# Up product: ten tiles in seven products instead of eight

## The chip, the cores and the metric

The kernel runs on one core of a Trainium2 chip. A core has five engines with a queue each: TensorE (PE in the profile; its weight loads are shown apart as PEld), VectorE (DVE), ScalarE (ACT), GpSimd (POOL) and SyncE (SP, which here only issues transfers). They wait for each other by semaphores. Matmul results land in PSUM, which has eight banks of 128 x 512 float32; everything else is in SBUF.

The metric is the device time of one execution in microseconds (us), as the median of several runs.

## The reference

One layer on x (1, 512, 1024) in float32: a mixing part (retention and a gated unit), then a gated MLP with a short convolution. The change touches the MLP:

```python
def _conv_gated_mlp(h, w_up, conv_w, conv_b, w_down):
    hid = h @ w_up                       # (512, 1024) @ (1024, 5632)
    hid = conv_general_dilated(hid, conv_w, ...) + conv_b   # 3 positions, each column by itself
    a, b = jnp.split(hid, 2, axis=-1)
    return (jax.nn.gelu(a) * b) @ w_down # (512, 2816) @ (2816, 1024)

h2 = _rmsnorm(x, g_pre_ffn)
x = x + _rmsnorm(_conv_gated_mlp(h2, w_up, conv_w, conv_b, w_down), g_post_ffn)
```

## The kernel before

**Number format.** Each operand is split into a high part (`hi`, rounded by an ACT copy, L85) and a low part (`lo`, the rest, by a DVE subtraction, L92). One product is three matmuls: high by high, high by low, low by high (`mm3`, L230).

**The up product.** Its 5632 columns are 22 tiles of 2 x 128: tile i holds the columns a and b that `gelu(a) * b` needs, as weight blocks 2i and 2i+1 of 128 x 1024 (eight pieces of 128 along the contraction). The result is held transposed, 128 columns by 512 positions.

A *whole* tile is two `up_block` calls (L954). Each takes one block (two slots, `hi` and `lo`) and one PSUM bank, and issues 8 x 3 matmuls of 512 columns: 48 matmuls of 512 for a tile.

A tile as a *pair* (class `Pair`, L675) is computed in the manner of Strassen and Winograd: seeing the two blocks, the two halves of the contraction and the two halves of the positions as a 2 x 2 product, it takes seven products of half the size in place of eight. Each is 4 x 3 matmuls of 256 columns: 84 matmuls of 256 for a tile. It needs weight forms B11, B21, T1 to T4 and B22 (`w_form`, L159), one slot each. T1 and T3 are sums made by DVE (L170, L171), T2 and T4 by POOL (L172, L174). Each of the seven forms is then split. On the other side stand forms of h2 (`h2forms`), made once.

A pair's seven products come in three parts, in three banks:
- `part1`: B11 into bank `b[0]` (ACT copies it out), B21 into `b[1]` (DVE adds it), T1 into `b[2]`, and T2 added into `b[0]`, which ACT copies out again (`copy(c1[:, T0], o)`, L711)
- `part2`: T3 added into `b[0]` (L717), ACT copies it out, DVE subtracts (L719). It also fetches the weights of the next part.
- `part3`: T4 added into `b[0]`, copied out by ACT; B22 added into `b[2]`, DVE subtracts (L731)

**The order around it.** `COUPLES` (L42) names eight couples of tiles, 4 to 19. In a couple the first tile is a pair and the second is whole: `part1`, first block, `part2`, second block with `part3` in its middle. Tiles 0 to 3, 20 and 21 are whole. After a tile `tile_done` (L1043) runs the convolution (ACT L997, DVE L1000 and L1004, for a and for b), the gelu (ACT L1011) and the product (DVE L1013). After tiles 7, 11, 13, 17 and 19 it also calls `down_forms` (L1024), which makes the operand forms of one pair of tiles for the down product: on DVE five steps of 256 and three of 512, on ACT four copies.

**Weights.** `units` (L99 to L123) lists what is prepared, in order: `("blk", i)` a block, `(form, i)` a form. `w_get` (L220) hands out the next unit and lets units be issued ahead up to nine slots (tag `w4`, nine buffers, L130). Loads go to `raw` tiles of 512 KB (four buffers, L127), issued by SP. `_up` (L1291) lays out the blocks of pair tiles in halves on the host.

**Who sets the order.** The program is handed to a framework that finds the dependencies, places tiles in free buffers of their tag and sets the order of each engine's instructions. The order written in the code is a priority there, not a fixed sequence. Temporaries (`tmp`) have six buffers, PSUM eight.

Of the kernel before, what the change touches and what calls it, by code (L numbers as in the profile page):

```python
# [38 lines left out]
ENDS = (0, 2, 3, 1)  # L39
UP0 = DOWN0 - 2 * NF  # L40
EARLY = 4
COUPLES = [(i, i + 1) for i in range(4, 20, 2)]  # L42

PRE, LNG, LNB = 0, 8, 16
CW, CB = 24, 24 + 3 * 2 * NF
# [5 lines left out]
def tile_block(ctx: ExitStack, tc, xT, x, wall, par, cs, wsp, bsp, gpost, gpre, gffn, out):  # L51
# [11 lines left out]
    def blk(dt=F32, n="blk", shape=(P, S)):  # L63
        return sb.tile(list(shape), dt, tag="blk", bufs=NBLK, name=nm(n))
# [4 lines left out]
    def tmp(n="tmp", shape=(P, S)):  # L69
        return sb.tile(list(shape), F32, tag="tmp", bufs=6, name=nm(n))  # L70
# [7 lines left out]
    def ps(shape=(P, S)):  # L78
        return pp.tile(list(shape), F32, tag="ps", name=nm("ps"))
# [18 lines left out]
    FORMS = ("B11", "B21", "T1", "T2", "T3", "T4", "B22")  # L98
    units = []  # L99
    i = 0  # L100
    while i < NW:
        pair = [(f, i) for f in FORMS]
        if U0 <= i < GATE0:
            units += pair
            i += 2
        elif GATE0 <= i < GATE1:
            units += pair[:4] + [("blk", i + 2)] + pair[4:] + [("blk", i + 3)]
            i += 4
        elif i == UP0 + 2 * COUPLES[0][0]:
            for a, b in COUPLES:  # L110
                pair = [(f, UP0 + 2 * a) for f in FORMS]
                units += pair[:4] + [("blk", UP0 + 2 * b)] + pair[4:] + [("blk", UP0 + 2 * b + 1)]
            i = UP0 + 2 * COUPLES[-1][1] + 2
        elif i == DOWN0:
            for _ in range(2):
                pairs = [[("q", i + j), ("t", i + j)] for j in range(DP)]
                whole = [[("blk", i + DP)], [("blk", i + DP + 1)]]
                for u in pairs[:4] + whole[:1] + pairs[4:6] + whole[1:] + pairs[6:] if i == DOWN0 else pairs + whole:
                    units += u
                i += DP + WHOLE // 2  # L120
        else:
            units.append(("blk", i))
            i += 1  # L123
# [90 lines left out]
    def w_next():  # L214
        u = units[w_pos[1]]
        w_ready[w_pos[1]] = w_unit(u)
        w_pos[1] += 1
        return w_size(u)

    def w_get(look=LOOK, most=99):  # L220

        i = w_pos[0]
        w_pos[0] += 1
        room = 2 * look + (2 if w_size(units[i]) == 2 else 0)
        n = sum(w_size(u) for u in units[i : w_pos[1]])
        while w_pos[1] < len(units) and (w_pos[1] <= i or n + w_size(units[w_pos[1]]) <= min(most, max(room, 9 if look == LOOK else 0))):
            n += w_next()
        return w_ready.pop(i)

    def mm3(o, ah, al, bh, bl, start, stop):  # L230
        nc.tensor.matmul(o, ah, bh, start=start, stop=False)  # L231
        nc.tensor.matmul(o, ah, bl, start=False, stop=False)  # L232
        nc.tensor.matmul(o, al, bh, start=False, stop=stop)  # L233
# [48 lines left out]
    for k in range(KD):  # L282
# [18 lines left out]
        for m in range(8):  # L301
            c = slice(m * P, (m + 1) * P)
# [78 lines left out]
    for m in range(8):  # L381
        t = blk(n="qkraw")
# [266 lines left out]
    for n, acc in enumerate(t_group()):  # L649
        if n == 0:  # L650
            g_turn(0)
        if n < 2:
            for k in (n + 2, n + 6):
                t = tmp("xT")
# [92 lines left out]
    uT, late = [], None  # L747
    for j in range(KD // 2):
        p = Pair(AF.Gelu_apprx_tanh, lambda: blk(n="u"), scale=rbc)
# [7 lines left out]
        late = p  # L757
# [46 lines left out]
    for j in range(KD // 2):  # L804
        for o, t in gated_pair(ogh, ogl, late if j == 0 else None):
            b = blk(n="r")
# [117 lines left out]
    def h2(k, t):  # L924
        return tuple(h[k // 2][:, k % 2, t] for h in (h2h, h2l))

    h2forms = {n: [None] * 4 for n in ("S1", "S2", "S3", "S4")}
# [8 lines left out]
    def h2_sums(i):  # L936

        a0, b0, a1, b1 = h2r[0][i], h2r[0][i + 2], h2r[1][i], h2r[1][i + 2]
        v.tensor_sub(b1, a1, b1)
        v.tensor_sub(a1, a0, a1)  # L940
        v.tensor_sub(a0, b1, a0)
        v.tensor_add(b0, b0, a0)
        for n, t in zip(("S1", "S2", "S3", "S4"), (b1, a0, a1, b0)):
            h2_parts(n, i, t)
# [9 lines left out]
    def up_block(between=None):  # L954
        (wh, wl), o = w_get(), ps()
        for k in range(KD):
            if between and k == KD // 2:
                between()
            c = slice(k * P, (k + 1) * P)
            mm3(o, wh[:, c], wl[:, c], *h2(k, slice(0, S)), k == 0, k == KD - 1)  # L960
        return o
# [33 lines left out]
    def conv(o, m):  # L995
        c = tmp("cv")
        nc.scalar.activation(  # L997
            out=c, in_=o, func=AF.Identity, scale=col(CW + 3 * m + 1), bias=col(CB + m)
        )
        v.scalar_tensor_tensor(  # L1000
            out=c[:, 1:S], in0=o[:, 0 : S - 1], scalar=col(CW + 3 * m), in1=c[:, 1:S],
            op0=ALU.mult, op1=ALU.add,
        )
        v.scalar_tensor_tensor(  # L1004
            out=c[:, 0 : S - 1], in0=o[:, 1:S], scalar=col(CW + 3 * m + 2), in1=c[:, 0 : S - 1],
            op0=ALU.mult, op1=ALU.add,
        )
        return c

    def gated(ca, cb):  # L1010
        nc.scalar.activation(out=ca, in_=ca, func=AF.Gelu_apprx_tanh)  # L1011
        gp.append(blk(n="gp"))
        v.tensor_mul(gp[-1], ca, cb)  # L1013
# [10 lines left out]
    def down_forms(j):  # L1024

        a, b = gp[2 * j], gp[2 * j + 1]
        first = blk(F32R, "fa")
        split(first[:, T0], first[:, T1], a[:, T0])
        s_ = blk(n="fs")
        v.tensor_sub(s_[:, T0], a[:, T1], b[:, T1])  # L1030
        v.tensor_sub(s_[:, T1], s_[:, T0], a[:, T0])
        v.tensor_sub(a[:, T0], a[:, T0], a[:, T1])
        v.tensor_add(a[:, T1], b[:, T0], s_[:, T1])
        bh, bl = two_parts(b, j >= WIDE)
        sh, sl = two_parts(s_, j >= WIDE)
        th, tl = two_parts(a, j >= WIDE)
        dforms.append({
            "A11": (first[:, T0], first[:, T1]), "A12": (bh[:, T0], bl[:, T0]), "A22": (bh[:, T1], bl[:, T1]),
            "S1": (sh[:, T0], sl[:, T0]), "S2": (sh[:, T1], sl[:, T1]),
            "S3": (th[:, T0], tl[:, T0]), "S4": (th[:, T1], tl[:, T1]),  # L1040
        })

    def tile_done(i, o):  # L1043
        gated(*(conv(t, 2 * i + s_) for s_, t in enumerate(o)))
        if i < COUPLES[-1][1]:
            if i in (7, 11, 13, 17):
                down_forms(len(dforms))
        elif len(dforms) < EAGER:
            down_forms(len(dforms))

    couples = dict(COUPLES)
    i = 0
    while i < NF:
        if i in couples:
            p = Pair(None, lambda: tmp("c"), h2, h2forms)
            p.part1()
            o = [up_block()]
            p.part2()
            o.append(up_block(p.part3))
            tile_done(i, p.t)  # L1060
            tile_done(i + 1, o)
            i += 2
        else:
            o = []
            for e in (2 * i, 2 * i + 1):
                o.append(early_o[e] if e < EARLY else up_block())
            if i < 2:
                h2_sums(i)
                w_next()
            tile_done(i, o)  # L1070
            i += 1
# [154 lines left out]
    for t in ENDS:  # L1226
# [10 lines left out]
        for i, (b, e) in enumerate((((M2, e1), (M3, xx)), ((M4, uu), (M8, yy)))[t // 2]):  # L1237
            f, h = slice((t % 2) * 256, (t % 2 + 1) * 256), slice(i * 256, (i + 1) * 256)
# [14 lines left out]
        if t in ADDED:  # L1253
            o = blk(n="o")
# [35 lines left out]

def _up(a):  # L1291

    for i, _ in COUPLES:
        b, c = a[2 * i].reshape(P, 2, S), a[2 * i + 1].reshape(P, 2, S)
        a[2 * i : 2 * i + 2] = np.stack([
            np.concatenate([b[:, 0], c[:, 0]], -1), np.concatenate([c[:, 1], b[:, 1]], -1),
        ])
    return a
# [85 lines left out]
```

## Time and profile before

| | us |
|---|---|
| median of 3 runs | 818.92 |
| lowest, highest | 818.67, 819.13 |
| the profiled execution | 818.99 |
| its span | 817.2 |
| PE busy | 810.2 |
| DVE busy | 657.0 |
| ACT busy | 430.0 |

The span runs from the first to the last instruction that the profile shows; the execution's time has some more around it. Start times in a view are in us from the start of the span. The up product lies between about 471 and 703 us, tiles 4 to 19 between 517 and 681. Matmuls are pipelined: a matmul of 256 columns is shown with 0.28 us, but the next starts about 0.11 later, so PE's pace is read from starts, not from durations. Some matmul records are missing from the trace.

In a row of a view, `wf<-raw` names the tile written and the tiles read: `wf` is the high or low part of a form, `wh` and `wl` those of a block, `c` a pair's result, `cv` a convolution's, `ps` a PSUM bank. `[1.71 <-PE ps L691]` says that the engine had been idle for 1.71 us until that instruction of PE released it.

### The profile page before, as it was taken

How to read it: one execution, taken by the hardware profiler on the slowest of the kernel's cores; microseconds unless marked ns; L12 is line 12 of the kernel's file. 1: busy time of each engine (PE TensorE's matmuls, PEld its weight loads, DVE VectorE, ACT ScalarE, POOL GpSimd, SP SyncE). 2: the span in 40 equal slices, each digit the busy share in tenths (PEclk: the TensorE clock that was granted, in tenths of full speed). 3: DMA queues.
4: the chain of work that ended last, by engine and by line, in shares of the span. 5: the costliest groups of instructions: out<-in, count | busy, mean ns of one | idle time of the engine just before them, and what ended most of it. 6: DMA issues, size and time to landing. Idle time of an engine off the chain costs nothing.

```text
span 817.2 us, 13212 instructions
## 1 busy us (share of the span) xinstructions
PE 810.2 (99%) x5154; PEld 730.9 (89%) x5154; DVE 657.0 (80%) x1076; ACT 430.0 (53%) x733; POOL 102.5 (13%) x108
## 2 busy tenths in 40 slices
PE   9999999999999999999999999999999999999997
PEld 7888888888899999999988898899999998999996
DVE  7579897877898877767766579778989989898976
ACT  6636445536665544444435466455656665645532
POOL 0100000012222011132211210210201200000001
PEclk9999999999999999999999999999999999999999
DMA  8733221222234332323359212333333341234354
GB/s 284 262 117 103 77 79 65 68 75 79 91 101 133 104 93 88 103 86 103 102 175 360 87 49 73 104 103 103 104 104 103 103 140 67 78 103 129 104 181 104
DMA packets 29391, 93.76 MB, mean 115 GB/s; under 512 B 3408, under 2 KB 4304, under 8 KB 29328
## 3 DMA queue, kind: packets, MB, share of 16 engines
q1 hardware_dynamic: 26928, 86.59, 32.1%
q0 software_dynamic: 1968, 6.03, 2.4%
q8 instruction: 40, 0.66, 0.4%
q10 hardware_dynamic: 432, 0.30, 0.1%
q14 instruction: 23, 0.19, 0.1%
HBM read 88.19 MB, written 4.72 MB: 114 GB/s over the span
## 4 chain that ended last, share of the span: by engine, by line
PE 98%; DMA 0%; DVE 0%; issue 0%; ACT 0%; DVEq 0%
PE ps L691 23%; PE ps L232 13%; PE ps L231 13%; PE ps L233 13%; PE ps L1088 11%; PE ps L495 5%; PE ps L496 5%; PE ps L497 5%; PE ps L1119 2%; PE ps L846 2%; PE ps L845 2%; PE ps L847 2%; PE ps L770 1%; PE ps L295 1%; PE ps L912 0%; PE ps L620 0%
## 5 line engine op out<-in xcount | busy, mean ns | idle before, releaser
L92 DVE TENSOR_TENSOR wl<-raw,wh 128x1024 fp32r<-128x1024 f32 (+1 forms) x93 | 108.9, 1180 | 48.2 <-PE ps L691 24.2
L85 ACT ACTIVATE wf<-raw 128x512 fp32r<-128x512 f32 x140 | 84.9, 626 | 98.7 <-PE ps L232 40.2
L92 DVE TENSOR_TENSOR wf<-raw,wf 128x512 fp32r<-128x512 f32 x140 | 110.0, 802 | 26.4 <-ACT wf L85 25.6
L691 PE MATMUL ps<-sh,wf 128*128 128x256 f32 x640 | 118.8, 277 | 0.0
L85 ACT ACTIVATE wh<-raw 128x1024 fp32r<-128x1024 f32 (+2 forms) x95 | 93.0, 989 | 34.5 <-DMA raw<-wall 16.5
L691 PEld LDWEIGHTS ps<-sh,wf 128*128 128x128 f32 x640 | 100.7, 188 | 0.9 <-ACT wf L85 0.2
L231 PE MATMUL ps<-h2h,wh 128*128 128x512 f32 (+1 forms) x256 | 93.2, 364 | 0.0
L232 PE MATMUL ps<-h2l,wh 128*128 128x512 f32 (+1 forms) x256 | 93.1, 364 | 0.0
L233 PE MATMUL ps<-h2h,wl 128*128 128x512 f32 (+1 forms) x256 | 92.8, 362 | 0.0
L691 PE MATMUL ps<-sl,wf 128*128 128x256 f32 x320 | 88.5, 277 | 0.0
L495 PE MATMUL ps<-wh,xh 128*128 128x512 f32 x192 | 75.1, 391 | 0.0
L496 PE MATMUL ps<-wl,xh 128*128 128x512 f32 x192 | 74.9, 390 | 0.0
L497 PE MATMUL ps<-wh,xl 128*128 128x512 f32 x192 | 74.8, 390 | 0.0
L172 POOL TENSOR_TENSOR raw<-raw,raw 128x512 f32<-128x512 f32 x20 | 33.9, 1693 | 239.5 <-DVE raw L170 185.9
L691 PEld LDWEIGHTS ps<-sl,wf 128*128 128x128 f32 x320 | 60.1, 188 | 0.8 <-issue 0.2
L233 PEld LDWEIGHTS ps<-h2h,wl 128*128 128x128 f32 x256 | 48.3, 189 | 7.7
L231 PEld LDWEIGHTS ps<-h2h,wh 128*128 128x128 f32 x256 | 48.2, 188 | 6.9
L232 PEld LDWEIGHTS ps<-h2l,wh 128*128 128x128 f32 x256 | 48.1, 188 | 6.5
L691 PE MATMUL ps<-xh,wf 128*128 128x256 f32 x288 | 53.4, 278 | 0.0
L1088 PE MATMUL ps<-dl,fh 128*128 128x256 f32 x168 | 46.5, 277 | 0.0
L1088 PE MATMUL ps<-dh,fl 128*128 128x256 f32 x168 | 46.5, 277 | 0.0
L1088 PE MATMUL ps<-dh,fh 128*128 128x256 f32 x168 | 46.5, 277 | 0.0
(326 smaller groups left out, 2057.9 us busy)
## 6 DMA issues: line engine op xcount, KB each, us to landing
raw<-wall SPq DMA_DIRECT2D x145, 512.0 KB, 3.5
x<-x SPq DMA_DIRECT2D x20, 256.0 KB, 5.5
xT<-xT SPq DMA_DIRECT2D x8, 256.0 KB, 5.5
x<-x POOLq DMA_DIRECT2D x8, 256.0 KB, 2.6
xT<-xT POOLq DMA_DIRECT2D x4, 256.0 KB, 3.9
cs<-cs SPq DMA_DIRECT2D x2, 256.0 KB, 4.2
gpm<-gpost POOLq DMA_DIRECT2D x2, 256.0 KB, 3.9
gpr<-gpre POOLq DMA_DIRECT2D x2, 256.0 KB, 5.0
```

Of the source, the lines that this page charges most:

```text
L85: nc.scalar.activation(out=o, in_=i, func=AF.Copy)
L92: return nc.vector.tensor_sub(lo, src, as32(hi))
L172: nc.gpsimd.tensor_tensor(out=w_raw["T2"], in0=w_raw["T1"], in1=w_raw["B22"], op=ALU.add)
L231: nc.tensor.matmul(o, ah, bh, start=start, stop=False)
L232: nc.tensor.matmul(o, ah, bl, start=False, stop=False)
L233: nc.tensor.matmul(o, al, bh, start=False, stop=stop)
L495: nc.tensor.matmul(acc[t], xh[k][:, c], wh[:, f], start=k == 0, stop=False)
L496: nc.tensor.matmul(acc[t], xh[k][:, c], wl[:, f], start=False, stop=False)
L497: nc.tensor.matmul(acc[t], xl[k][:, c], wh[:, f], start=False, stop=k == KD - 1)
L691: nc.tensor.matmul(o, w_[:, c], a_, start=first and k == n == 0, stop=k == 3 and n == 2, skip_group_check=True,)
L845: nc.tensor.matmul(o, ah, bh, start=k == 0, stop=False)
L1088: nc.tensor.matmul(o, a_[:, c], w_[:, f], start=j == t == i == 0, stop=j == DP - 1 and i == 2 and n not in (M2, M3, M4), skip_group_check= ...
```

## The change

- `COUPLES` becomes `GROUPS`: four groups of three tiles (4 to 6, 7 to 9, 10 to 12, 13 to 15) and two couples (16, 17) and (18, 19). In a group of three the first two tiles are pairs and the third is whole. So ten tiles are pairs: 4, 5, 7, 8, 10, 11, 13, 14, 16, 18.
- The order in a group of three: first pair's `part1`, `part2`; second pair's `part1`; first pair's `part3` and `tile_done`; second pair's `part2`; first block of the whole tile; second block with the second pair's `part3` in its middle; `tile_done` for both. In the first pair `part2` follows `part1` with nothing between them.
- `units` lists 7 + 7 forms and then the two blocks for a group of three. For a couple it is as before.
- `down_forms` comes after tiles 9, 12, 15 and 17 (`SUMS_AT`) and 19, instead of 7, 11, 13, 17 and 19.
- `_up` lays out the blocks of all ten pair tiles.

```diff
-COUPLES = [(i, i + 1) for i in range(4, 20, 2)]
+GROUPS = [(i, i + 1, i + 2) for i in range(4, 16, 3)] + [(16, 17), (18, 19)]
+SUMS_AT = (9, 12, 15, 17)
...
-        elif i == UP0 + 2 * COUPLES[0][0]:
-            for a, b in COUPLES:
-                pair = [(f, UP0 + 2 * a) for f in FORMS]
-                units += pair[:4] + [("blk", UP0 + 2 * b)] + pair[4:] + [("blk", UP0 + 2 * b + 1)]
-            i = UP0 + 2 * COUPLES[-1][1] + 2
+        elif i == UP0 + 2 * GROUPS[0][0]:
+            for *a, b in GROUPS:
+                for t in a:
+                    units += [(f, UP0 + 2 * t) for f in FORMS]
+                units.insert(len(units) if a[1:] else len(units) - 3, ("blk", UP0 + 2 * b))
+                units.append(("blk", UP0 + 2 * b + 1))
+            i = UP0 + 2 * GROUPS[-1][-1] + 2
...
-        if i < COUPLES[-1][1]:
-            if i in (7, 11, 13, 17):
+        if i < GROUPS[-1][-1]:
+            if i in SUMS_AT:
                 down_forms(len(dforms))
...
-    couples = dict(COUPLES)
+    groups = {g[0]: g for g in GROUPS}
     i = 0
     while i < NF:
-        if i in couples:
+        if i in groups:
             p = Pair(None, lambda: tmp("c"), h2, h2forms)
             p.part1()
-            o = [up_block()]
-            p.part2()
+            if len(groups[i]) > 2:
+                p.part2()
+                late, p = p, Pair(None, lambda: tmp("c"), h2, h2forms)
+                p.part1()
+                late.part3()
+                tile_done(i, late.t)
+                i += 1
+                p.part2()
+                o = [up_block()]
+            else:
+                o = [up_block()]
+                p.part2()
             o.append(up_block(p.part3))
             tile_done(i, p.t)
             tile_done(i + 1, o)
...
-    for i, _ in COUPLES:
+    for i in (t for g in GROUPS for t in g[:-1]):
```

## The prediction

> **What bounds the kernel now.** I read the page first, then TensorE's waits.
>
> ```profile
> span 817.2 us, 13212 instructions
> PE 810.2 (99%) x5154; PEld 730.9 (89%) x5154; DVE 657.0 (80%) x1076; ACT 430.0 (53%) x733; POOL 102.5 (13%) x108
> ...
> PE 98%; DMA 0%; DVE 0%; issue 0%; ACT 0%; DVEq 0%
> ```
>
> ```profile
> PE ps L280 <- DVE raw L275: 1.0, 1, 1.0
> ```
>
> PE is busy for 99% of the span, the chain that ended last is PE for 98%, and the second fence is the whole list of PE's waits: one, 1.0 us, at the start. So PE has no wait anywhere in the up product. Time can be won there only by giving PE less to do, and lost by making it wait.
>
> Next the windows view over the up product. Columns: window, its length, then busy time (instructions) of PE, PEld, DVE, ACT, POOL, then clock and DMA.
>
> ```profile
> 517.00:537.50 20.50, 20.50 (x133) 18.57 (x132) 13.88 (x20) 10.49 (x19) 2.93 (x2) 1.00 0.28 96
> 537.50:558.00 20.50, 20.50 (x133) 18.57 (x132) 15.70 (x25) 11.20 (x20) 2.94 (x2) 1.00 0.32 103
> 558.00:578.50 20.50, 20.50 (x133) 18.57 (x132) 19.85 (x32) 12.70 (x23) 2.94 (x2) 1.00 0.28 87
> 619.50:640.00 20.50, 20.50 (x133) 18.57 (x132) 20.05 (x32) 12.47 (x24) 2.94 (x2) 1.00 0.32 96
> 681.00:702.80 21.80, 21.80 (x98) 18.04 (x97) 19.36 (x33) 11.36 (x17) 0.00 (x0) 1.00 0.17 54
> ```
>
> The first four rows are couples: one tile in seven products (a pair) and one whole tile, 20.50 us each, PE never idle. In a couple without `down_forms` DVE is busy for 15.70 us, in one with them for 19.85 to 20.05. The last row is tiles 20 and 21, both whole: 10.9 us each.
>
> **What the change saves on PE.** The chain in order of time gives the pieces of a pair (start, length, matmuls):
>
> ```profile
> 537.69 5.45 PE ps L691 x48
> 548.60 1.37 PE ps L691 x12
> 552.71 2.73 PE ps L691 x24
> ```
>
> ```profile
> 221.94 38.04 PE ps L691 x335
> ```
>
> A pair is 48 + 12 + 24 = 84 matmuls, 5.45 + 1.37 + 2.73 = 9.55 us. The last fence is the U stage, four pairs in a row: 38.04 / 335 = 0.1136 us a matmul, so pairs that follow each other cost no more. In a couple the whole tile then takes 20.50 - 9.55 = 10.95 us. Tiles 4 to 15 are six couples now, 6 x 20.50 = 123.0. After it they are four groups of 2 x 9.55 + 10.95 = 30.05, together 120.2. **Saved on PE: 2.8 us** (2.7 with the 10.9 of tiles 20 and 21). Tiles 16 to 19 and the down product keep their work and their order.
>
> **What the other engines get.** The groups of instructions by line, for 480 to 690 us (count, busy, mean ns):
>
> ```profile
> L92 DVE TENSOR_TENSOR wf<-raw,wf 128x512 fp32r<-128x512 f32 x56 | 42.4, 771 | 6.6 <-ACT wf L85 5.8
> L92 DVE TENSOR_TENSOR wl<-raw,wh 128x1024 fp32r<-128x1024 f32 x24 | 31.9, 1327 | 12.9 <-PE ps L691 7.6 <-issue 5.1 <-ACT wh L85 0.3
> L85 ACT ACTIVATE wf<-raw 128x512 fp32r<-128x512 f32 x56 | 34.2, 626 | 25.3 <-PE ps L232 11.8 <-POOL raw L172 6.2 <-DVE raw L171 3.8
> L85 ACT ACTIVATE wh<-raw 128x1024 fp32r<-128x1024 f32 x23 | 24.2, 1053 | 0.1
> L85 ACT ACTIVATE c<-ps 128x256 f32<-128x256 f32 x32 | 12.1, 379 | 26.5 <-PE ps L691 26.5
> L171 DVE TENSOR_TENSOR raw<-raw,raw 128x512 f32<-128x512 f32 x8 | 6.3, 782 | 0.2
> L170 DVE TENSOR_TENSOR raw<-raw 128x512 f32<-128x512 f32 x8 | 5.5, 690 | 0.0
> L719 DVE TENSOR_TENSOR c<-ps,c 128x256 f32<-128x256 f32 x8 | 3.4, 420 | 0.1
> ```
>
> A tile that turns from whole to pair adds on DVE seven `wf` subtractions, two sums of weights and three 256-wide steps, and drops two `wl`: 7 x 0.771 + 0.782 + 0.690 + 3 x 0.42 - 2 x 1.327 = 5.5 us. On ACT: 7 x 0.626 + 4 x 0.379 - 2 x 1.053 = 3.8 us. POOL gets two more additions per pair. SP issues the same two transfers of 512 KB per tile.
>
> With 15.70 for a couple, whole = (15.70 - 5.5) / 2 = 5.1 and pair = 10.6. A group is 26.3 us of DVE, and with `down_forms` (19.85 - 15.70 = 4.15) 30.5, against 30.05 of PE. The new `SUMS_AT` puts `down_forms` into the second, third and fourth group and couple (16, 17). DVE falls behind by about 0.4 us a group, 1.2 in all; couple (16, 17), 19.85 of 20.50, gives back 0.65. ACT has at most 12.7 + 8 of 30.
>
> What hides this is the lead of the weights:
>
> ```profile
> 574.67 2.00 DVE L92 TENSOR_TENSOR wl<-raw,wh 128x1024 fp32r<-128x1024 f32 x1 [0.46 <-PE ps L691]
> ```
>
> ```profile
> 583.97 0.39 PE L231 MATMUL ps<-h2h,wh 128*128 128x512 f32 x1
> ```
>
> This `wl` is ready at 576.67 and first used at 583.97, 7.3 us ahead. After it the shortest way is that of a second pair's first form: with nine slots held, its slot is free when the group before ends, and its matmuls come 6.8 us into the group. A copy, a subtraction and a sum (0.63 + 0.77 + 0.78) leave over 4 us for a lag of 1 to 2. The U stage says the same:
>
> ```profile
> 225.70:235.00 9.30, 9.30 (x84) 9.30 (x84) 9.20 (x15) 6.67 (x12) 1.80 (x2) 1.00 0.31 104
> ```
>
> In these 9.30 us DVE is busy for 9.20, and PE still has no idle time: a nearly full DVE doesn't by itself hold PE up.
>
> **The new wait.** In a couple a whole block stands between `part1` and `part2`. In a group of three the first pair's `part2` follows at once, and its product adds into the bank, `b[0]`, that `part1` has just filled and ACT must copy out (`copy(c1[:, T0], o)`). PE can't write until the copy is done. No row shows such a wait, so it is bounded: nothing below (a copy hidden by other matmuls), above by the copy's own rows.
>
> ```profile
> 542.86 0.28 PE L691 MATMUL ps<-sh,wf 128*128 128x256 f32 x1
> 542.97 0.40 PE L231 MATMUL ps<-h2h,wh 128*128 128x512 f32 x1
> ```
>
> ```profile
> 543.17 0.38 ACT L85 ACTIVATE c<-ps 128x256 f32<-128x256 f32 x1 [1.71 <-PE ps L691]
> ...
> 563.67 0.38 ACT L85 ACTIVATE c<-ps 128x256 f32<-128x256 f32 x1 [1.41 <-PE ps L691]
> ```
>
> The last product of `part1` issues at 542.86, the next matmul at 542.97, the copy ends at 543.55: 0.58 us. For the signal back I add 0.07, about twice the 0.03 from the last matmul's end (542.86 + 0.28) to the copy's start: 0.65. Four groups: 2.6 us, nearly all of the gain. Behind the waiting matmul stand the second pair's products, and the whole chain.
>
> Whether it is paid turns on PE's order. The framework sets each engine's order by what it reckons ready, as DVE shows:
>
> ```profile
> 537.15 0.75 DVE L1000 SCALAR_TENSOR_TENSOR cv<-c,part,cv 128x511 f32<-128x511 f32 x1
> 537.81 0.74 DVE L1000 SCALAR_TENSOR_TENSOR cv<-ps,part,cv 128x511 f32<-128x511 f32 x1
> 538.57 0.69 DVE L92 TENSOR_TENSOR wf<-raw,wf 128x512 fp32r<-128x512 f32 x1
> 539.17 0.74 DVE L1004 SCALAR_TENSOR_TENSOR cv<-c,part,cv 128x511 f32<-128x511 f32 x1
> ```
>
> The code has L1004 right behind L1000 for one tile; here the next tile's L1000 and a weight split go between, because L1004 wasn't ready. If PE is ordered so too, some five matmuls of the second pair's first product (0.11 us each, another bank, weights ready) move ahead of the waiting one and fill the gap. I take this, with 0.15 us left over per group, since the planned length of the copy need not be the real one: 4 x 0.15 = 0.6 (ends 0 and 2.6).
>
> [...]
>
> **Sum.** -2.8 + 0.6 = -2.2 us: span 815.0. The profiled execution took 818.99, 1.8 beyond its span, and stands 0.07 above the median: 816.8, against the median **816.7 us**. With 0 to 0.35 left per group, 816.1 to 817.5.
>
> **The rivals.**
> 1. *The wait is paid in full.* PE keeps the written order. For: no case of moved matmuls in the trace. Against: DVE's order above. -2.8 + 2.6: 818.7 (818.3 to 818.9), no change.
> 2. *The wait, and a split ahead of the copy*, the case on the slower side. In the U stage:
>
> ```profile
> 228.48 0.28 PE L691 MATMUL ps<-xh,wf 128*128 128x256 f32 x1
> ```
>
> ```profile
> 228.74 0.63 ACT L85 ACTIVATE wf<-raw 128x512 fp32r<-128x512 f32 x1 [0.74 <-PE ps L691]
> 229.28 0.37 ACT L85 ACTIVATE u<-ps 128x256 f32<-128x256 f32 x1
> ```
>
> `part1` ended at 228.48, but ACT did a split first, as the same matmul freed its slot, and the copy ended at 229.65: 1.2 us. In four groups 4.8 - 2.8 = +2.0: 820.9. With written order it is slower by over 0.2% from 1.1 us a wait. Against it: in the couples (543.17, 563.67) ACT stood idle and copied at once.
> 3. *DVE becomes the bound.* From the second group on it has 30.5 for 30.05, and in the first group the second pair's forms are wanted 6.8 us after the start instead of 20.5. If POOL's additions hold DVE longer than now, the lag outgrows 4 us. The 2.00 of the `wl` at 574.67 stands beside
>
> ```profile
> 574.29 1.30 POOL L174 TENSOR_TENSOR raw<-raw,raw 128x512 f32<-128x512 f32 x1 [1.47 <-DVE wf L92]
> ```
>
> and is 0.7 over the mean of its form. With 1.1 us more per pair, three groups reach 32.7: 8 late, less 4 of lead, less 2.8: +1.2, 820; 1 or 2 lost give 818 to 819. [...]
>
> **Chances.** Forecast 0.62, rival 1 0.20, rival 2 0.07, rival 3 0.11 (a third each faster, same, slower). 0.2% is 1.64 us, about what a measurement of this kernel can tell from no change: faster is under 817.3, slower over 820.6. Faster 0.61 + 0.03 = 0.64, same 0.01 + 0.20 + 0.04 = 0.25, slower 0.07 + 0.04 = 0.11. The range covers the forecast and rival 1: 816.0 to 818.9, some 0.85.
>
> **What would show it.** Right: four stretches of 30.1 to 30.3 us between the groups' first products, a few matmuls of the second pair ahead of L717's product, PE's waits at L691 under 1.4 us in all. Rival 1: L691 waiting for ACT `c` four times, 0.6 each. Rival 2: a `wf` or `wh` copy right ahead of that `c` copy. Rival 3: PE waiting for DVE `wf` or `wl`, most in the third and fourth group. Wrong altogether: a pair that takes other than 9.55 us.

## The result, and the profile after

The kernel after takes **826.48 us** (826.12 to 827.65), the kernel before 818.78 us beside it: a ratio of 1.0095 [1.0084, 1.0107]. It is slower by 7.7 us where 2.2 us faster was forecast. The page of the kernel after (span and instructions, busy time by engine, the engines' shares of the chain that ended last):

```profile
span 824.4 us, 13423 instructions
PE 811.3 (98%) x5226; PEld 733.3 (89%) x5226; DVE 667.8 (81%) x1096; ACT 435.9 (53%) x751; POOL 111.3 (13%) x112
...
PE 19%; DVE 3%; issue 3%; ACT 2%; POOL 1%; DVEq 0%; POOLq 0%; ACTq 0%
```

The chain was PE for 98%. Now it goes through DVE, ACT and POOL as well (the shares add up to 28%, because the view follows this chain back only to 594 us). TensorE's waits in the up product of the kernel after (us in total, times, longest; L694 is L691 of before, a pair's product):

```profile
PE ps L694 <- ACT c L86: 4.6, 7, 1.5
PE ps L694 <- DVE wf L93: 1.4, 2, 0.8
```

PE waits most for ACT's `c` copies, the ones that empty a pair's bank, and little for weights (DVE `wf`). The windows view of the kernel after, the four groups and the first couple (window, length, busy time of PE, PEld, DVE, ACT, POOL with counts, clock, DMA):

```profile
516.72:547.50 30.78, 30.76 (x217) 28.65 (x216) 23.56 (x34) 18.03 (x32) 7.20 (x5) 1.00 0.29 98
547.50:578.63 31.13, 30.76 (x217) 28.65 (x216) 27.30 (x42) 18.57 (x35) 5.87 (x4) 1.00 0.31 102
578.63:611.60 32.97, 31.03 (x218) 28.48 (x216) 29.18 (x48) 18.53 (x36) 5.63 (x3) 1.00 0.29 97
611.60:646.50 34.90, 31.49 (x218) 28.75 (x216) 32.72 (x51) 20.65 (x38) 7.01 (x4) 1.00 0.23 78
646.50:667.00 20.50, 20.50 (x134) 18.56 (x132) 20.03 (x31) 13.07 (x23) 2.95 (x2) 1.00 0.30 100
```

Each group was to take 30.05 us. The third and fourth take 32.97 and 34.90; they are the two in which DVE does most. Together the groups lose 0.73 + 1.08 + 2.92 + 4.85 = 9.6 us; the couples and tiles 20 and 21 behind them lose 0.6 more and the saved products give 2.8 back, so the stage of tiles 4 to 21 is 7.4 us longer. These two rows, of the kernel before and of the kernel after, give that stage as a whole; below, "the stage" means this window:

```profile
517.02:702.78 185.76, 185.76 (x1153) 166.57 (x1152) 162.14 (x250) 108.88 (x182) 20.56 (x14) 1.00 0.32 102
```

```profile
516.72:709.87 193.15, 187.12 (x1225) 169.80 (x1224) 172.70 (x268) 114.83 (x199) 28.66 (x18) 1.00 0.29 98
```

How a late DVE reaches PE shows in the timeline of the kernel after, at the start of group 4 (start, length, engine, what it waited for):

```profile
612.15 1.73 POOL L175 TENSOR_TENSOR raw<-raw,raw 128x512 f32<-128x512 f32 x1 [2.49 <-DVE c L734]
...
612.63 2.46 DVE L1003 SCALAR_TENSOR_TENSOR cv<-c,part,cv 128x511 f32<-128x511 f32 x2
615.01 0.74 DVE L1007 SCALAR_TENSOR_TENSOR cv<-c,part,cv 128x511 f32<-128x511 f32 x1
...
615.84 0.63 ACT L1014 ACTIVATE cv<-cv 128x512 f32<-128x512 f32 x1 [1.02 <-DVE cv L1007]
616.37 0.61 ACT L86 ACTIVATE wf<-raw 128x512 fp32r<-128x512 f32 x1
616.89 0.36 ACT L86 ACTIVATE c<-ps 128x256 f32<-128x256 f32 x1
...
617.31 0.39 PE L694 MATMUL ps<-sh,wf 128*128 128x256 f32 x1 [1.46 <-ACT c L86]
```

Read it downwards. A POOL addition runs from 612.15 to 613.88. DVE's two L1003, 0.74 us each when alone, take 2.46 together. So the convolution of the last group's tiles ends late, at 615.75. ACT stands with its GELU at the head of its queue and waits 1.02 us for it. Behind the GELU stand a weight split and then the copy of the pair's bank. Its product had ended by 614.49, and ACT had nothing to do from 614.82 on, so the copy could have run 2 us earlier but for the order of the queue. The copy ends at 617.25, and PE, which must add into that bank, has waited 1.46 us.

### The profile page after: what moved, and what is told of

Read it like the earlier page. It is cut to its first block, busy times and chain, and to the rows that moved or that the text cites. A ratio compares the mean times of both kernels' runs of the same rounds, so it can differ in the third digit from the quotient of the medians.

```text
span 824.4 us, 13423 instructions
## 1 busy us (share of the span) xinstructions
PE 811.3 (98%) x5226; PEld 733.3 (89%) x5226; DVE 667.8 (81%) x1096; ACT 435.9 (53%) x751; POOL 111.3 (13%) x112
## 5 line engine op out<-in xcount | busy, mean ns | idle before, releaser
L86 ACT ACTIVATE wf<-raw 128x512 fp32r<-128x512 f32 x154 | 93.4, 625 | 113.2 <-PE ps L235 30.2
L93 DVE TENSOR_TENSOR wf<-raw,wf 128x512 fp32r<-128x512 f32 x154 | 118.4, 785 | 32.3 <-ACT wf L86 32.1
L694 PE MATMUL ps<-sh,wf 128*128 128x256 f32 x704 | 133.0, 279 | 6.0 <-ACT c L86 4.6
L694 PEld LDWEIGHTS ps<-sh,wf 128*128 128x128 f32 x704 | 111.3, 188 | 8.7 <-ACT c L86 6.2
L694 PE MATMUL ps<-sl,wf 128*128 128x256 f32 x352 | 97.6, 277 | 0.0
L234 PE MATMUL ps<-h2h,wh 128*128 128x512 f32 (+1 forms) x224 | 80.5, 360 | 0.0
L235 PE MATMUL ps<-h2l,wh 128*128 128x512 f32 (+1 forms) x224 | 80.4, 359 | 0.0
L236 PE MATMUL ps<-h2h,wl 128*128 128x512 f32 (+1 forms) x224 | 80.3, 358 | 0.0
L694 PEld LDWEIGHTS ps<-sl,wf 128*128 128x128 f32 x352 | 66.1, 188 | 0.6 <-issue 0.2
L175 POOL TENSOR_TENSOR raw<-raw,raw 128x512 f32<-128x512 f32 x22 | 36.3, 1651 | 193.9 <-DVE raw L173 107.9
L694 PE MATMUL ps<-xh,wf 128*128 128x256 f32 x288 | 53.4, 278 | 0.0
L177 POOL TENSOR_TENSOR raw<-raw,raw 128x512 f32<-128x512 f32 x22 | 32.5, 1477 | 119.3 <-DVE wf L93 119.3
L234 PEld LDWEIGHTS ps<-h2h,wh 128*128 128x128 f32 x224 | 42.1, 188 | 5.9
L1101 PE MATMUL ps<-dh,fh 128*128 128x256 f32 x168 | 46.5, 277 | 0.0
L1101 PE MATMUL ps<-dl,fh 128*128 128x256 f32 x168 | 46.4, 276 | 0.0
```

The source lines that it names most:

```text
L86: nc.scalar.activation(out=o, in_=i, func=AF.Copy)
L93: return nc.vector.tensor_sub(lo, src, as32(hi))
L175: nc.gpsimd.tensor_tensor(out=w_raw["T2"], in0=w_raw["T1"], in1=w_raw["B22"], op=ALU.add)
L177: nc.gpsimd.tensor_tensor(out=w_raw["T4"], in0=w_raw["T2"], in1=w_raw["B21"], op=ALU.add)
L694: nc.tensor.matmul(o, w_[:, c], a_, start=first and k == n == 0, stop=k == 3 and n == 2, skip_group_check=True,)
L1101: nc.tensor.matmul(o, a_[:, c], w_[:, f], start=j == t == i == 0, stop=j == DP - 1 and i == 2 and n not in (M2, M3, M4), skip_group_check= ...
```

## The experiments

Three theories. **A**: the down forms' work on DVE makes it late, and ACT's queue passes it on. **B**: the handover from pair to pair (the new wait) costs it. **C**: the two GpSimd additions of a pair (T2 and T4) do it, either because ACT and DVE wait for them (C2) or because DVE is slower beside them (C1). Every edit below is against the kernel after; where an edit adds lines, the line numbers of the rows shift by a few (L697 is L694 of after, L1006 its L1003, L737 its L734). The stage takes TensorE 183.0 us without any loss (185.76 - 2.8). A stage is read from the one execution that was profiled; in runs 1 and 5 this lay 2.3 and 1.4 us under the median.

**1. The forms late.**

```diff
-SUMS_AT = (9, 12, 15, 17)
+SUMS_AT = (17, 18)
```

> The changed kernel with SUMS_AT = (17, 18): no down_forms in the four groups; the five calls come after tiles 17 to 21. Nothing is left out. Theory A (DVE gets late in the groups that carry down_forms; ACT's queue, in order, waits for it with a gelu, and the copies that free a pair's bank stand behind): the waits of PE for ACT's c copies in groups 2 to 4 shrink to those of group 1 (30.8 us a group), so about 819 us, 818 to 821. Theory B (the loss is the bank handed from part1 to part2 with nothing between, and DVE's load is beside the point): nothing changes in the groups, 824 to 827 us.

The whole: 828.77 us (826.49 to 829.43), ratio 1.0118 [1.0102, 1.0133], over the ranges of both theories. But its stage is 186.61 us, 6.5 less than after. What was won there was lost behind it: the rest of the span takes 121.67 us, 114.53 in after. Part of that stands in the waits of TensorE at the down product (L1101):

```profile
PE ps L1101 <- ACT dh L86: 3.5, 4, 1.2
PE ps L694 <- ACT c L86: 1.4, 4, 0.4
```

The forms had only been moved in front of a product that needs DVE as much. The total can't judge theory A here; the stage speaks for it.

**2. The whole tile's first block between the two parts of the first pair**, as in the couples of before.

```diff
-                units.insert(len(units) if a[1:] else len(units) - 3, ("blk", UP0 + 2 * b))
+                units.insert(len(units) - 7 * len(a) + 4, ("blk", UP0 + 2 * b))
...
             p.part1()
+            o = [up_block()]
             if len(groups[i]) > 2:
                 p.part2()
...
-                p.part2()
-                o = [up_block()]
-            else:
-                o = [up_block()]
-                p.part2()
+            p.part2()
```

> The changed kernel with the whole tile's first block between the first pair's part1 and part2, as in a couple, so that 5.5 us of other matmuls stand before the product that adds into the copied bank; down_forms as in the changed kernel. Theory A: the handover of the bank costs at most the 0.2 to 0.7 us that each group shows ahead of L720's product, so 823 to 825.5 us, and the waits at the second product of part1 stay. Theory B: most of the loss goes, 816 to 818 us.

828.12 us, ratio 1.0109 [1.0092, 1.0126], over the ranges of both theories. B falls as the main cause: the handover is covered, and two longer waits for the same kind of copy, 7.4 us together, stand elsewhere. In its timeline ACT's rows ahead of the longest, and PE's:

```profile
595.50 1.15 ACT L86 ACTIVATE wf<-raw 128x512 fp32r<-128x512 f32 x2 [1.69 <-POOL raw L177]
596.55 1.04 ACT L86 ACTIVATE wh<-raw 128x1024 fp32r<-128x1024 f32 x1
597.50 0.36 ACT L86 ACTIVATE c<-ps 128x256 f32<-128x256 f32 x1
...
597.91 0.58 PE L694 MATMUL ps<-sh,wf 128*128 128x256 f32 x1 [3.98 <-ACT c L86]
```

Again ACT's order: the copy stood behind splits, the first of which waited for a GpSimd sum (L177).

**3. Both edits.**

> The edits of the two kernels before together: no down_forms in the groups, and a block between part1 and part2. Theory A: groups near their 30.05 us of PE work, 816 to 818 us, faster than the kernel before. Theory B: the same as with the block alone. If DVE is then late in couples (16, 17) and (18, 19) and at tiles 20 and 21, which now carry all five down_forms, 818 to 821 us with PE's waits there.

827.94 us, ratio 1.0113 [1.0098, 1.0128], outside the ranges of theory A, with the down product late as in 1. Its stage is 185.58 us, still 2.6 over TensorE's own time though no forms stand in the groups.

**4. T4 on VectorE**: `nc.vector.tensor_add` for the T4 addition of the up product.

> The changed kernel with the addition for T4 of the up product's pairs on DVE instead of POOL. Theory C (ACT's queue waits for POOL's T4 addition, 1.7 to 2.2 us long, with the bank copies behind it): the two waits of 0.85 and 0.87 us at 596.39 and 631.29 go and ACT waits less for POOL, 822 to 825 us. If only the amount of DVE work counts: 0.7 us more of it for each of ten pairs, less what POOL took from DVE, so the same or slower, 826 to 829 us.

826.79 us, ratio 1.0096 [1.0081, 1.0111]: no gain. Half of the additions had stayed on GpSimd, and between 615 and 622 us a single T2 kept it busy for 3.12 us (1.54 on the mean in after). TensorE's waits moved to the weights, and the longest was followed by a lower clock (last section):

```profile
PE ps L697 <- DVE wf L93: 4.0, 2, 3.4
```

Next, parts were left out, so that nothing is moved to another stage.

**5. Three of the four sets of forms left out** (the first set is used four times).

```diff
-SUMS_AT = (9, 12, 15, 17)
+SUMS_AT = (17,)
...
                 down_forms(len(dforms))
+                dforms.extend(dforms * 3)
```

> After's order, with three of the four sets of down forms left out of the computation (the first set, made at tile 17, is used four times), so that VectorE and ScalarE have nothing but the up product's own work in the four groups and the down product begins with the load it has in after. Theory A (the forms' VectorE work delays ScalarE's queue, and with it the copies of the pairs' banks): stage of the up tiles 4 to 21 at about 186.6 us, as where the forms came late, against 193.15 in after, and as nothing is shifted into the down product the whole at 819 to 820.5 us. If the loss is in the handover from pair to pair itself: the stage stays above 191 us and the whole above 824.

820.70 us, ratio 1.0022 [1.0011, 1.0033], just over theory A's range; stage 186.13, as expected there.

**6. The additions left out of the up product**, forms as in after.

```diff
+            if i >= UP0:
+                w_raw["T2"] = w_raw["T4"] = w_raw["B21"]
+            else:
                 nc.gpsimd.tensor_tensor(out=w_raw["T2"], in0=w_raw["T1"], in1=w_raw["B22"], op=ALU.add)
-        elif form == "T4":
+        elif form == "T4" and i < UP0:
```

> After's order, with GpSimd's two additions a pair (T2 and T4) left out of the up product (other loaded weights stand in their place); the down forms stay where after has them. Theory C (the loss goes through the GpSimd additions: VectorE's splits beside them take 835 instead of 687 ns, and ScalarE's copies wait 2 to 2.7 us for a GpSimd sum): the stage of the up tiles falls to 186 to 188 us, the whole to 819 to 822. If the amount of the forms alone counts (Theory A without the additions' part): above 190 us and above 824.

817.45 us, ratio 0.9990 [0.9981, 1.0000], better than its own theory's bound. The windows view of this run, the four groups:

```profile
516.61:546.91 30.30, 30.28 (x218) 28.17 (x217) 23.08 (x37) 17.60 (x32) 0.00 (x0) 1.00 0.25 89
546.91:577.21 30.30, 30.28 (x218) 28.17 (x217) 25.68 (x42) 18.54 (x34) 0.00 (x0) 1.00 0.31 104
577.21:607.51 30.30, 30.28 (x218) 28.17 (x217) 28.69 (x50) 20.50 (x37) 0.00 (x0) 1.00 0.32 105
607.51:637.81 30.30, 30.28 (x218) 28.17 (x217) 27.66 (x47) 20.70 (x37) 0.00 (x0) 1.00 0.35 121
```

All the forms are there, DVE is busy for up to 28.69 us of a group, and each group takes 30.30. In this run, where GpSimd does nothing, the forms cost the groups nothing.

**7. Both left out**, and **8. both left out, with the block between** (the edits of 5 and 6, then of 2).

> After's order, with both left out: three of the four sets of down forms, and GpSimd's two additions a pair in the up product. By theories A and C together nothing is late but the handover in the pairs: the stage of the up tiles at 183.5 to 185 us (182.96 is TensorE's own work), the whole at 816.5 to 818. If a further loss remains (handover, matmuls at a longer pitch behind a wait): above 818.

> As the run with both left out, and the whole tile's first block stands between the two parts of the first pair, as it does in the couples of before. If the handover costs what its waits show (some 1.8 us over four groups): 0.5 to 1.8 us under the run with both left out, the whole at 816 to 816.7, which is TensorE's saving of 2.8 us and nothing else. If the block between costs more than it hides: over the run with both left out.

Run 7: 817.23 us, ratio 0.9982 [0.9972, 0.9991], stage 183.96, the same as in run 6. Run 8: 815.63 us, ratio 0.9955 [0.9927, 0.9983], stage 182.84, a little better than its range. So TensorE's saving is real (185.76 - 182.84 = 2.9 us in the stage), and the handover costs 183.96 - 182.84 = 1.1 us over four groups. The losses of the stage do not add up from parts: forms alone nothing (6 against 7), additions alone 2.2 us (5 against 7), both 9.2 (after against 7). By the medians of the whole it is 0.2, 3.5 and 9.2. Neither does it alone; the loss takes both.

**9 and 10. Does DVE wait for the additions, or run slower beside them?** In run 9 T4 is made right behind T2, into the place of B11, so that it need not wait for T2's split; in run 10 both additions run and nothing reads them.

```diff
             nc.gpsimd.tensor_tensor(out=w_raw["T2"], in0=w_raw["T1"], in1=w_raw["B22"], op=ALU.add)
+            if i >= UP0:
+                w_raw["T4"] = w_raw["B11"]                        # run 9 only
+                nc.gpsimd.tensor_tensor(out=w_raw["T4"], in0=w_raw["T2"], in1=w_raw["B21"], op=ALU.add)
+                w_raw["T2"] = w_raw["T4"] = w_raw["B21"]          # run 10 only
-        elif form == "T4":
+        elif form == "T4" and i < UP0:
```

> After's order and all of its work; GpSimd makes T4 right behind T2, into the place of B11 (split by then), where after makes it in T2's own place and must wait until VectorE has split T2 (the row: GpSimd's T4 addition waited 61.7 us in ten pieces for VectorE's split in the stretch of the up tiles). Theory C2 (the loss comes by the wait: ScalarE's copy of T4 stands in its queue for the late addition, and the banks' copies behind it): ScalarE's waits of 2 to 2.7 us for that addition go, the stage of the up tiles 4 to 21 falls from 193.15 to under 187 us, the whole to under 821. Theory C1 (the loss comes by contention: VectorE's work beside the additions takes longer, 835 instead of 687 ns a split, and VectorE is late): the additions cost VectorE the same as before, the stage stays over 190 us and the whole over 824.

> After's order; GpSimd makes both additions of each pair of the up product, but nothing reads them (the forms T2 and T4 are left out of the computation, a loaded weight stands in their place). So the contention is there and the wait isn't. Theory C1 (contention): stage over 188 us, whole over 821.5, with VectorE's splits at 760 ns or more on the mean, as in after. Theory C2 (wait): stage at 184 to 184.6 us as without the additions, whole at 817.4 to 818.3, whatever VectorE's splits take.

Run 10: 825.30 us, ratio 1.0080 [1.0065, 1.0095]. Apart from the additions, TensorE, VectorE and ScalarE have the same instructions in the same order as in run 6, so the difference of 7.9 us comes from additions that nobody reads. The group of weight splits on DVE, by line and form, in run 6 and then in run 10 (count, busy, mean ns):

```profile
L93 DVE TENSOR_TENSOR wf<-raw,wf 128x512 fp32r<-128x512 f32 x63 | 42.2, 685 | 8.5 <-ACT wf L86 8.4
```

```profile
L93 DVE TENSOR_TENSOR wf<-raw,wf 128x512 fp32r<-128x512 f32 x63 | 54.6, 883 | 0.0
```

And the stage of run 6, then of run 10:

```profile
516.61:700.57 183.96, 183.88 (x1226) 167.82 (x1224) 162.10 (x267) 115.29 (x198) 0.00 (x0) 1.00 0.30 101
```

```profile
516.75:708.95 192.20, 186.88 (x1225) 169.73 (x1224) 179.67 (x270) 115.59 (x199) 30.33 (x18) 1.00 0.29 99
```

DVE is busy for 179.67 - 162.10 = 17.6 us more, over 18 additions: **1.0 us of DVE per GpSimd addition of 1.7 us** in this run. How, is in the timeline of run 10, two additions of POOL and what DVE does meanwhile:

```profile
576.08 1.72 POOL L175 TENSOR_TENSOR raw<-raw,raw 128x512 f32<-128x512 f32 x1 [8.80 <-DMA raw<-wall]
577.88 1.63 POOL L177 TENSOR_TENSOR raw<-raw,raw 128x512 f32<-128x512 f32 x1
...
576.57 1.79 DVE L93 TENSOR_TENSOR wf<-raw,wf 128x512 fp32r<-128x512 f32 x1
578.28 0.41 DVE L737 TENSOR_TENSOR c<-ps,c 128x256 f32<-128x256 f32 x1
578.61 1.44 DVE L1006 SCALAR_TENSOR_TENSOR cv<-c,part,cv 128x511 f32<-128x511 f32 x1
579.98 0.68 DVE L93 TENSOR_TENSOR wf<-raw,wf 128x512 fp32r<-128x512 f32 x1
```

The split at 576.57 begins inside the addition, which ends at 577.80, and ends 0.56 us after it, nearly its own length of 0.68. The same holds for L1006: the addition ends at 579.51, L1006 at 580.05, 0.54 later. Only L737, which reads one of its inputs from a bank (`ps`), runs at its usual 0.41 beside the second addition. The means of the stage, run 6 and then run 10, go the same way: 685 and 883 ns for the splits and 746 and 847 for L1006 with a `c` tile, whose inputs are all in SBUF; 743 and 741 for L1006 with a bank, 419 and 414 for L737.

Run 9: 822.37 us, ratio 1.0043 [1.0026, 1.0060], stage 190.12. Taking the wait for T4 away wins 4.1 us of the 7.7, though DVE is busier (177.62 us in the stage, 172.70 in after). ACT's waits for the T4 sum, 11.5 us in after, are 0.5 us there. So both ways are there and C1 does not hold alone: DVE's instructions are longer with the additions (a split 795 ns on the mean, 685 in run 6), and the late sums cost once more through ACT's queue. What an addition costs DVE is not the same in each run. Against run 6 the same 18 additions cost DVE 10.6 us in after (172.70 - 162.10), 15.5 in run 9 and 17.6 in run 10: 0.59, 0.86 and 0.98 us each. How much of run 10's loss is DVE's longer instructions, and how much that loaded weights are held until their additions are done, that run can't part.

**11. Both additions on VectorE.**

> After's order and all of its work; both additions of each pair of the up product on VectorE instead of GpSimd. VectorE then has four additions a group more than without them (4 x 0.69 = 2.8 us on top of 28.7 and 27.7 us in groups 3 and 4 of 30.3) and no other engine beside it. If VectorE's amount decides: groups 1 and 2 at 30.3, groups 3 and 4 at 31 to 32, the stage at 185.5 to 188 us, the whole at 819 to 822. If only the GpSimd additions' lateness and contention count: the stage under 184.6, the whole under 818.3.

820.50 us, ratio 1.0024 [1.0015, 1.0034], stage 187.06. Each addition costs DVE 0.69 us there, about what each one on GpSimd took from it in after (0.59). The stage of this run, then its groups 3 and 4:

```profile
516.69:703.75 187.06, 186.09 (x1225) 168.63 (x1224) 173.38 (x287) 116.09 (x199) 0.00 (x0) 1.00 0.29 102
```

```profile
577.33:608.92 31.59, 31.35 (x217) 28.64 (x216) 30.82 (x53) 19.53 (x37) 0.00 (x0) 1.00 0.29 101
608.92:641.00 32.08, 31.43 (x218) 28.51 (x217) 31.68 (x54) 21.65 (x39) 0.00 (x0) 1.00 0.27 96
```

DVE fills 98 and 99% of these two, and each is about as long as DVE needs; groups 1 and 2 of the same run (DVE 24.7 and 27.9) took 30.34 and 30.30. The first row says what the amount of DVE's work can't explain: DVE is busy for 173.38 us, no less than in after (172.70), and yet the stage is 6.1 us shorter. So of after's 9.2 us, some 6 come from having the sums on GpSimd, and not from how much DVE has to do.

**12. The early T4 with the block between.**

> The early T4, and the whole tile's first block between the two parts of the first pair, with all of the work. With the block between alone PE waited 4.0 us in one piece for a copy on ScalarE and the whole came to 828. If the late addition is what holds ScalarE (C2): no wait over 1 us for a copy, the stage at 183 to 185 us, the whole at 816 to 818, faster than the kernel before. If contention keeps VectorE late (C1): over 822.

826.60 us, ratio 1.0095 [1.0080, 1.0110], far from the first range and in the second: TensorE waited 2.6 us in one piece for a copy. With the block between, the additions start in other places; DVE's splits took 900 ns on the mean. In this order the early T4 doesn't help; why it does in run 9 and not here, no run shows.

**13 to 15. The forms in halves**: `down_forms` is cut into its sums (with the first split) and its three other splits, some 2.1 us each, at successive tiles. Run 13 has the additions on VectorE, run 14 the block between as well, run 15 the additions on GpSimd with the early T4.

```diff
-SUMS_AT = (9, 12, 15, 17)
+SUMS_AT = {6: "a", 9: "b", 12: "a", 15: "ba", 17: "ba", 19: "b"}
...
-        if i < GROUPS[-1][-1]:
-            if i in SUMS_AT:
-                down_forms(len(dforms))
-        elif len(dforms) < EAGER:
+        for part in SUMS_AT.get(i, ""):
+            (down_a if part == "a" else down_b)(len(dforms))
+        if i >= GROUPS[-1][-1] and len(dforms) < EAGER:
```

> All of the work, after's order of the products; both additions of a pair on VectorE, and each set of down forms made in two halves of some 2.1 us at successive tiles (6 and 9, 12 and 15, 15 and 17, 17 and 19) in place of whole sets of 4.2 us at 9, 12, 15 and 17. In the run with the additions on VectorE the groups had VectorE at 24.7, 27.9, 30.8 and 31.7 us against 30.3 of TensorE. If VectorE's amount in a group is the cause that remains: 24.7, 27.5, 29.5, 29.5 or so in the groups, none over 30.3, the groups at 30.3 each, the stage of the up tiles at 184 to 185 us against 187.06, and the whole at 817.4 to 818.8, level with the kernel before or under it. If ScalarE's queue or the order made for TensorE is what is late in groups 3 and 4: no better than 820.

> The same, and the whole tile's first block stands between the two parts of the first pair. If VectorE's amount is the cause: 0.25 us a group less again (183 to 184 us in the stage), the whole at 816.3 to 818.2. If a late VectorE remains: a wait for a copy in one piece, as the block between had alone (4.0 us), and the whole over 820.

> All of the work, after's order; GpSimd keeps the additions, T4 made early, and the down forms in halves as in the run with the additions on VectorE. If the GpSimd additions' cost to VectorE (18 additions took 17 us of VectorE's time in the run that left them unread) is as much as the work moved: VectorE still over 30 us in groups 2 to 4, the stage at 185.5 to 188.5, the whole at 819.5 to 822. If the spread alone suffices: under 818.8.

Run 13: 818.99 us, 1.0007 [0.9998, 1.0015], stage 185.53. Run 14: 818.46 us, 0.9997 [0.9988, 1.0006], stage 185.17. Both level with the kernel before, just over the range expected: group 4 of run 13 still had

```profile
608.54:639.88 31.34, 31.22 (x218) 28.77 (x216) 30.52 (x51) 19.74 (x36) 0.00 (x0) 1.00 0.28 100
```

Run 15: 823.06 us, 1.0061 [1.0049, 1.0073], stage 190.07 against 190.12 in run 9, so the spread alone mends nothing with GpSimd at work; both lie above the range expected.

**16 and 17. Two groups only** (4 to 9), with the block between and the additions on VectorE there; couples from 10 on with GpSimd's additions.

```diff
-GROUPS = [(i, i + 1, i + 2) for i in range(4, 16, 3)] + [(16, 17), (18, 19)]
-SUMS_AT = (9, 12, 15, 17)
+GROUPS = [(4, 5, 6), (7, 8, 9)] + [(i, i + 1) for i in range(10, 20, 2)]
+SUMS_AT = (9, 11, 13, 17)          # run 17: (9, 11, 15, 17)
```

> All of the work: only tiles 4 to 9 in two groups (the block between the two parts of the first pair, both additions of a pair on VectorE), tiles 10 to 19 in couples with GpSimd's additions as in the kernel before, whole sets of down forms at tiles 9, 11, 13 and 17. One saved product more than before costs TensorE 1.4 us less (two groups 60.1 where three couples are 61.5). If VectorE's amount is all that decides (two groups at 24.7 and some 26 of 30, couples at 20.1 of 20.5): 817.2 to 817.8, faster than the kernel before by 0.15% or so. If three couples in a row with a set of forms each make VectorE late: 818.5 or more.

> The two groups and five couples again, with the third set of down forms at tile 15 in place of 13, so that no three couples with a set follow each other. In the run before it the couples from 617.76 and 638.61 us took 20.85 and 21.20 us in place of 20.50, 1.05 us together, with VectorE at 20.4 of the first. If it is VectorE's amount over three couples in a row: the couples at 20.50, the stage of the up tiles 4 to 21 at 184.3 us against 185.35, and the whole at 817.0 to 817.5, faster than the kernel before. If it is anything else in those couples: 818 or more.

Run 16: 818.20 us, 0.9992 [0.9983, 1.0001], between its two ranges; its groups took 30.02 us each, but two couples were late behind three sets of forms in a row:

```profile
576.76:597.26 20.50, 20.50 (x133) 18.56 (x132) 20.05 (x32) 12.59 (x23) 2.95 (x2) 1.00 0.27 92
...
617.76:638.61 20.85, 20.84 (x134) 18.70 (x132) 20.39 (x32) 13.19 (x23) 2.96 (x2) 1.00 0.30 101
638.61:659.81 21.20, 20.82 (x134) 18.69 (x132) 18.78 (x29) 12.83 (x22) 2.95 (x2) 1.00 0.35 124
```

Run 17: **817.52 us**, 0.9984 [0.9975, 0.9993], against 818.85 beside it and at the edge of its range. With one set moved on, the stage is 184.63, the couples but one are back at 20.50 us (one took 20.8, where 20.50 was expected), and this version is faster than both kernels, by 1.3 us compared with the one before.

## Why the prediction was wrong

**Right: what TensorE saves.** 2.8 us were forecast; with nothing else late the stage fell by 2.9 (run 8). A pair takes 9.55 us beside another pair too.

**Right: the new wait and what fills it.** The forecast was some five matmuls of the second pair moved ahead and 0.15 us left. In run 6, where nothing else is late, four stand ahead and the gap is 0.18 us; in all the handover costs 0.28 us a group (1.1 / 4). Rivals 1 and 2, as priced, did not happen at the place they named: in after the same first wait is 0.18 to 0.67 us. What rival 2 described, a split right ahead of the copy, did happen, but at another product, T2 in `part1` (the wait that ends at 617.31).

**Nearly right: "a group is 26.3 us of DVE, and with `down_forms` ... 30.5".** Two more pairs were to bring DVE 2 x 5.5 = 11.0 us; in the stage it has 10.6 more (162.14 to 172.70). A group with forms has 28.69 us without GpSimd (run 6). With four additions at the 0.59 us of after that makes 31.05, an estimate, against TensorE's 30.05: a lag of 1.0 us a group where "about 0.4" was reckoned. The place was wrong too: forms that come after tile 9 run in the next group, so in after they start at 587 and 622 us, in the third and fourth group, and then in both couples. Rival 3 let the additions hold DVE longer, at a chance of 0.11. But its 1.1 us more per pair, a term that no run shows, did not come (the stage has 10.6 us more of DVE where 11.0 was reckoned), nor did its sign: PE waited 1.4 us for `wf` and 4.6 for `c` copies.

**Wrong: "what hides this is the lead of the weights ... over 4 us for a lag of 1 to 2", and "ACT has at most 12.7 + 8 of 30".** This is the step that failed, and for rival 3's price too, which took the same 4 us off. It took the weights for the only way by which a late DVE can reach PE, and so put a lag of 1 to 2 us at nothing. The lead of the weights did hold: PE waited 1.4 us for `wf` in all. But DVE's lag has a second way to PE. ACT's time was not the matter, its order was: splits, GELU and bank copies stand in one queue, the first two wait for DVE and POOL, and the copy that PE needs next stands behind them. That copy has no lead of weights; PE comes back to the bank two products later. The waits of the kernel before had shown ACT waiting for convolutions and for POOL sums, in the stage of the up tiles where DVE was on time:

```profile
ACT cv L1011 <- DVE cv L1004: 6.3, 4, 3.3
...
ACT wf L85 <- POOL raw L172: 5.4, 5, 1.2
```

The prediction did not ask what stood behind these. In the kernel after ACT waits 14.0 us in 12 pieces with a GELU for a convolution, 11.5 us in 5 with a split for a T4 sum and 3.7 us in 3 for a T2 sum. Such waits alone do not decide, though. In run 5, without the forms, they are as long (15.3 us in 14 pieces and 11.8 in 5), and PE waits only 1.1 us for copies.

"A nearly full DVE doesn't by itself hold PE up" was read from 9.3 us of the U stage. It holds in run 6 at 95% and not in run 11 at 98 to 99%.

**What stays open**: how the 6.1 us between after and run 11 part between sums that come late and DVE instructions that get longer at the wrong moment. Run 9 (no wait for T4: 3.0 us less in the stage) and run 11 (no GpSimd: 6.1 less) overlap, and each changes where DVE's work falls. The way through ACT's queue is read from timelines (617.31 in after, 597.91 in run 2); no run changed the order of that queue alone. And of the 10.2 us by which after's stage is over TensorE's own 183.0, 6.0 are PE's idle time (193.15 - 187.12). The other 4.2 lie in its busy time, in matmuls that start later than their pace; their causes were not followed one by one.

## What to carry to other kernels

Before taking work from the bounding engine, add up the next one over the stretch in which it gets more, with what another engine's work costs it: here 0.6 to 1.0 us of DVE for each GpSimd addition (0.59 in after, 0.98 in run 10). The amount is not all: with the same DVE time, sums that GpSimd made cost 6 us more than sums that DVE made in its own order. Then follow its lag through every in-order queue that waits for it and ask what stands behind the waiting instruction; cover counted for one consumer (the weights) says nothing of another (the bank copies). Where it doesn't fit, take less of the gain: two groups with an unfilled DVE were faster than the kernel before, four at best level with it.

## What the hardware showed beside that

In three runs TensorE ran at half its clock behind a wait. The windows of run 4, around its wait of 3.41 us that ended at 624.67 (the column behind POOL's is the granted clock):

```profile
622.00:626.00 4.00, 1.33 (x6) 1.33 (x7) 3.01 (x7) 3.17 (x7) 0.00 (x0) 0.72 0.01 4
626.00:629.00 3.00, 3.00 (x16) 3.00 (x16) 2.97 (x7) 0.67 (x2) 0.00 (x0) 0.50 0.11 19
629.00:632.50 3.50, 3.50 (x26) 3.50 (x26) 1.28 (x2) 2.67 (x5) 0.00 (x0) 0.77 0.80 250
```

At 0.50 a matmul of 256 columns takes 0.21 us of pitch in place of 0.114 (run 12, from 600 to 602 us), so the wait is paid for once more: 3.00 us at 0.50 and 3.50 at 0.77 hold some 2.3 us less work than at 1.00, an estimate from the last two rows. The same follows both waits of run 2: behind the one of 3.98 us the clock was 0.50 from 597.9 to 600 us, and behind the other, of 3.4 us, the page's slice from 620 to 641 us is the only one with a clock under 0.9. So the totals of these runs hold the lower clock too. In run 12 it followed shorter waits: behind 2.57 us the clock was 0.50 from 600 to 602 us, and behind 2.12 us it was 0.73 from 634 to 638 us, with matmuls at 0.21 us of pitch. In the kernel after, whose longest wait is 1.46 us, the groups' rows show 1.00.

A longer pitch stands behind some short waits too: in each of the first two groups of the kernel after, three matmuls of a pair's product took 0.356 us instead of 0.340 from the handover to the next 512-wide block, some 0.5 us a group. The wait alone isn't its cause: in run 6 the same wait of 0.18 us was followed by 0.340 us again within 1.5 us. What makes the difference stays open.
